# Retention in three parts: queries and keys, values, and the recurrence, with block products through DRAM

## The chip, the cores and the metric

The kernel runs on one core of a Trainium2 chip. The metric is the time on the device in microseconds (us) of one execution. TensorE (PE in the profile) multiplies, VectorE (DVE) and ScalarE (ACT) do elementwise work, GpSimd (POOL) does small things and issues DMAs of its own, SyncE (SP) issues the other DMAs.

## The reference, cut to what matters

One layer of a decoder trunk: 1024 positions, width 1024, all in float32. Both branches of the mixing sub-layer read `u`; the change is in the retention branch (4 heads, queries and keys of 256, values of 512).

```python
hq, hf, hi, hg, rq, rk, rv, rg, ga, gb = jnp.split(u @ w_in[l], split_at, axis=-1)
ya = _hgrn2(hq, hf, hi, hg, lower_bounds[l]) @ w_pa[l]
yb = _retention(rq, rk, rv, rg, positions) @ w_pb[l]
y = (jax.nn.sigmoid(ga) * ya + jax.nn.sigmoid(gb) * yb) @ w_o[l]
x = _layer_norm(DEEPNORM_ALPHA * x + (1.0 + gate1) * y, ln1_g[l], ln1_b[l])
u = x * (1.0 + scale2) + shift2
h = jnp.square(jax.nn.relu(u @ w_up[l] + b_up[l]))
x = _layer_norm(DEEPNORM_ALPHA * x + (1.0 + gate2) * (h @ w_down[l] + b_down[l]), ln2_g[l], ln2_b[l])

def _retention(q, k, v, g, positions):          # q, k rotated by position; per chunk of 128 positions:
    scores = jnp.einsum('bhid,bhjd->bhij', qc, kc) * decay_mask
    o = einsum('bhij,bhje->bhie', scores, vc) + einsum('bhid,bhde->bhie', qc * q_decay, state)
    state = chunk_decay * state + jnp.einsum('bhjd,bhje->bhde', kc * k_decay, vc)
    # then each head's output is centered, normalized and gated by silu(g)
```

## The kernel before

Every large product is float32 made of three: each operand is split by `split` into a part that TensorE reads as fp32r (ACT writes it, tile names ending in h) and a rest (DVE writes it, names ending in l), and `mm3` multiplies h by h, h by l and l by h into one PSUM tile. `u`, transposed, lies split in `uh`, `ul`, as four blocks `ub[j, hf]` (j: half of the width, hf: half of the positions).

The stages follow one another in `build`: `start` (modulation, `u`); the HGRN2 branch, whose dense products `h_dense(p)` are woven with the recurrence `h_pair_rec` of the heads before (`weave` emits steps of two generators in turn), with `gate_proj` of `ga` beside the last; the retention, head by head (`r_head`); `gates` (`gb`, `rg`); `merge`; `out_proj`; `ffn_up`; `ffn_down`.

Each `r_head` projects queries and keys (`dense_T`, 8 times 3 matmuls of 512 columns for one tile), rotates them on DVE, takes the scores of 128 by 128 positions, and then, for each half b of the value width, goes through 8 chunks of 128 positions: `r_v` projects the values of the next chunk (24 matmuls of 256 columns), the state in PSUM (`G`, L901) grows by key times value, and the output (L914) is scores times value plus query times the split state. Columns of the adaptive modulation are summed on DVE beside it (`ada_group`, L424 and L426, two 512 KB loads each, 16 groups in all).

`gates`, `merge`, `ffn_up` and `ffn_down` already use the scheme of Strassen and Winograd: a product of 2 by 2 blocks by seven block products q1 to q7, each on sums of blocks. The sums of the weights of `gb`, `rg`, `pa`, `pb`, `dn` are made in DRAM beforehand by accumulating DMAs (`block_sums`, 8 a part, started by POOL through `start_sums`, one after every so many matmul columns); those of `u` are made by `t_sums` on DVE. `product` and `products` run the block products, `group_out` adds their results up.

Weights come through one stream (`build_stream`, `W`): SP loads pieces of 512 KB into `raw` (three buffers, `raw_bufs`, L316), ACT and DVE split them into `wh`, `wl` (three buffers), and `W` keeps them ahead of the matmuls. The `ada` loads use the same three buffers. The program's order on each engine is set by a scheduler from this code.

## Time and profile before

| what | number |
|---|---|
| median of 3 runs | 2356.52 us (2353.17 to 2358.53) |
| profiled execution | 2359.06 us, of which span 2357.3 us |
| PE, DVE, ACT, POOL busy | 98%, 65%, 38%, 13% |
| mean granted TensorE clock | 0.995 |
| HGRN2 with `ga` | 45 to about 644 us |
| retention | about 644 to 1177 us |
| `gates`, `merge`, `out_proj` | to 1420, 1625, 1740 us |
| `ffn_up`, `ffn_down` | to 2050, 2357 us |

A matmul's row in the profile tells its whole passage through the array, and successive ones overlap; what one costs in a stream is the distance between two starts. DVE and ACT rows overlap only slightly. Every engine works through its own queue in order. Line numbers are those of the kernel before; in the changed kernel they stand a little off.

### The profile page before, as it was taken

The page shows a single profiled execution, that of the slowest core. Times are in us where ns is not written, and L with a number is a line of the kernel's source. Part 1 is how long each engine was busy: PE and PEld are TensorE (multiplying, and loading weights), DVE is VectorE, ACT ScalarE, POOL GpSimd, SP SyncE. Part 2 cuts the span into 40 slices and gives each one's busy share as a digit, 9 for nine tenths or more (in the row PEclk, how much of TensorE's full clock was granted, in tenths as well). Part 3 has the DMA queues.
Part 4 walks back from the last instruction along what each step waited for, and adds up shares of the span by engine and source line. Part 5 has one row for each costly group of instructions (what it writes and reads, how often), then busy time and mean ns, then how long its engine had stood idle before and what let it go on. Part 6 is the DMA issues. An engine that isn't in the chain of part 4 may idle for free.

```text
span 2357.3 us, 31812 instructions
## 1 busy us (share of the span) xinstructions
PE 2299.5 (98%) x12146; PEld 1968.0 (83%) x12146; DVE 1526.5 (65%) x2764; ACT 907.4 (38%) x1447; POOL 313.1 (13%) x479
## 2 busy tenths in 40 slices
PE   7999999999999999999989999999999999999998
PEld 5898888888789898999978878888887888888887
DVE  8356778777274756566576676657787565544678
ACT  4412223232223242424444444442455555544332
POOL 0111122212211121111231111000000000000000
PEclk9999999999999999999999999999999999999999
DMA  9555555545663655546476778776237475865674
GB/s 269 152 137 143 125 141 141 138 120 143 165 188 81 174 139 158 156 123 179 108 251 234 249 259 272 261 262 205 90 116 254 164 251 174 316 206 189 211 237 158
DMA packets 251304, 432.62 MB, mean 184 GB/s; under 512 B 14624, under 2 KB 154128, under 8 KB 245520
## 3 DMA queue, kind: packets, MB, share of 16 engines
q1 hardware_dynamic: 199568, 250.28, 32.9%
q0 software_dynamic: 51264, 179.86, 27.7%
q8 instruction: 95, 1.56, 0.3%
q14 instruction: 57, 0.47, 0.1%
q10 hardware_dynamic: 320, 0.45, 0.1%
HBM read 351.89 MB, written 162.54 MB: 218 GB/s over the span
## 4 chain that ended last, share of the span: by engine, by line
PE 86%; DVE 7%; DMA 4%; ACT 1%; issue 1%; POOL 1%; SPq 0%; DVEq 0%; POOLq 0%; ACTq 0%
PE psd L187 17%; PE psd L189 17%; PE psd L188 17%; PE psc L187 4%; PE psc L188 4%; PE psc L189 4%; PE psa L189 3%; PE psa L188 3%; PE psa L187 3%; PE psa L638 3%; PE psb L914 3%; PE psc L901 2%; PE psb L187 1%; PE psb L188 1%; PE psb L189 1%; DVE wl L183 1%
## 5 line engine op out<-in xcount | busy, mean ns | idle before, releaser
L183 DVE TENSOR_TENSOR wl<-raw,wh 128x1024 fp32r<-128x1024 f32 (+1 forms) x288 | 299.0, 1044 | 236.6 <-ACT wh L182 233.1
L182 ACT ACTIVATE wh<-raw 128x1024 fp32r<-128x1024 f32 (+1 forms) x288 | 262.2, 918 | 417.3 <-PE psd L188 227.5
L187 PE MATMUL psd<-uh,wh 128*128 128x512 f32 x788 | 316.1, 403 | 0.0
L188 PE MATMUL psd<-ul,wh 128*128 128x512 f32 x788 | 312.8, 397 | 0.4 <-DVE ul L183 0.4
L189 PE MATMUL psd<-uh,wl 128*128 128x512 f32 x788 | 313.1, 397 | 0.0
L187 PE MATMUL psd<-wh,uh 128*128 128x256 f32 x768 | 221.2, 288 | 0.0
L189 PE MATMUL psd<-wh,ul 128*128 128x256 f32 x768 | 218.2, 284 | 0.0
L188 PE MATMUL psd<-wl,uh 128*128 128x256 f32 x768 | 218.1, 284 | 0.0
L183 DVE TENSOR_TENSOR hl<-hr,hh 128x1024 fp32r<-128x1024 f32 x96 | 117.3, 1223 | 136.6 <-ACT hh L182 136.6
L188 PEld LDWEIGHTS psd<-ul,wh 128*128 128x128 f32 x788 | 149.0, 189 | 29.0 <-DVE ul L183 1.4
L189 PEld LDWEIGHTS psd<-uh,wl 128*128 128x128 f32 x788 | 148.8, 189 | 28.8
L187 PEld LDWEIGHTS psd<-uh,wh 128*128 128x128 f32 x788 | 148.8, 189 | 28.2 <-ACT uh L182 0.7
L182 ACT ACTIVATE hh<-hr 128x1024 fp32r<-128x1024 f32 x96 | 101.3, 1055 | 182.4 <-PE psb L188 68.0
L187 PEld LDWEIGHTS psd<-wh,uh 128*128 128x128 f32 x768 | 147.0, 191 | 3.0 <-issue 2.6
L188 PEld LDWEIGHTS psd<-wl,uh 128*128 128x128 f32 x768 | 147.0, 191 | 0.3
L189 PEld LDWEIGHTS psd<-wh,ul 128*128 128x128 f32 x768 | 147.0, 191 | 0.0
L645 DVE COPY_PREDICATED hS<-mask,psa 128x128 f32<-128x128 uint8 x288 | 75.8, 314 | 16.7 <-PE psa L638 14.5
L638 PE MATMUL psa<-qp,k 128*128 128x192 f32 x384 | 74.6, 334 | 8.4 <-DVE k L614 8.0
L871 DVE SCALAR_TENSOR_TENSOR vl<-psd,cst,vh 128x256 fp32r<-128x256 f32 x64 | 30.9, 483 | 78.1 <-ACT vh L870 78.1
L638 PEld LDWEIGHTS psa<-qp,k 128*128 128x128 f32 x384 | 63.3, 192 | 17.8 <-issue 14.6
L870 ACT ACTIVATE vh<-psd,cst 128x256 fp32r<-128x256 f32 x64 | 30.3, 473 | 117.5 <-PE psd L189 110.3
L187 PE MATMUL psd<-wh,hh 128*128 128x512 f32 x168 | 65.5, 390 | 0.9 <-ACT o L1405 0.9
(506 smaller groups left out, 5678.5 us busy)
## 6 DMA issues: line engine op xcount, KB each, us to landing
raw<-in_w_in SPq DMA_DIRECT2D x90, 512.0 KB, 4.9
raw<-in_w_up SPq DMA_DIRECT2D x66, 512.0 KB, 5.4
hr<-hv_d SPq DMA_DIRECT2D x56, 512.0 KB, 3.6
dn_s<-in_w_down POOLq DMA_DIRECT2D x48, 512.0 KB, 4.5
hv_d<-hv POOLq DMA_DIRECT2D x16, 1280.0 KB, 5.5
raw<-in_w_ada SPq DMA_DIRECT2D x32, 512.0 KB, 4.8
raw<-dn_s SPq DMA_DIRECT2D x32, 512.0 KB, 4.4
hr<-pv_d SPq DMA_DIRECT2D x28, 512.0 KB, 4.6
```

The source lines that it names most:

```text
L182: self.nc.scalar.activation(hi, src, AF.Copy)
L183: self.nc.vector.tensor_tensor(lo, src, hi.bitcast(F32), op=ALU.subtract)
L187: r = mm(out, wh, uh, start=start, stop=False, skip_group_check=more)
L188: mm(out, wh, ul, start=False, stop=False, skip_group_check=more)
L189: l = mm(out, wl, uh, start=False, stop=stop, skip_group_check=more)
L638: nc.tensor.matmul(pa[:, c * 192:(c + 1) * 192].rearrange("p (b w r) -> p b w r", w=2, r=3 * sz), k[:, n * P:(n + 1) * P], mv, start=True, ...
L645: V.copy_predicated(dst, self.mask8[:, o:o + 128].rearrange("p (b two s) -> p b two s", two=2, s=sz), src)
L870: nc.scalar.activation(hi, pd, AF.Copy, scale=sc)
L871: nc.vector.scalar_tensor_tensor(lo, pd, sc, hi.bitcast(F32), op0=ALU.mult, op1=ALU.subtract)
L901: mm(G[e], l[:, n % 2, es], r, start=n == 0 and i == 0, stop=i == 2, skip_group_check=n > 0)
L914: mm(po, l, r, start=i == 0, stop=i == len(pairs) - 1)
```

## The change

Queries and keys of all four heads are now one block product (`r_qk`: names `rq`, `rk`, 28 steps of 24 matmuls of 512 columns), rotated in `qk_block` (six DVE operations of 512 columns for each pair of an even and an odd tile) and written to DRAM (`qk_d`). Then the values of all heads follow (`r_values`: `rv0`, `rv1`, again 28 steps of 24), scaled and written to DRAM (`v_d`), with the 16 `ada_group`s beside them. Then `r_rec` runs the recurrence from these arrays by 256 positions: `r_prep(i)` loads, splits, transposes and scores one half of a head's positions while `r_main` does the half before. The weight sums of the four new products are 64 more DMAs in `block_sums`: 160 are started from the HGRN2 stage on (before: 96) and 64 later. The sums of `u` are made twice, by `u_sums` in `r_qk` and in `gates`, the second time with one block (`u12`) read back from DRAM. The rotation's angles (`rotary`) move from the second and third pair of HGRN2 heads to the first dense products.

```diff
+ADA_STEPS = (0, 1, 3, 5)
+QK_STEPS = group_steps([(n, p) for n in ("rq", "rk") for p in range(2)])
...
-    def r_qk(self, h):
-    def r_scores(self, h, hf):
-    def r_v(self, h, t, w):
-    def r_head(self, h):
-    def r_norm(self, h, n, of):
...
+    def qk_block(self, s, name, j, n, k, src, sign):
+        nc, V = self.nc, self.nc.vector
+        p, g = divmod(j, 2)
+        if src is s["X"]:
+            r = self.o_tile()
+            nc.scalar.activation(r, src, AF.Copy, scale=sign)
+            src, sign = r, 1.0
...
+        d = self.qk_d[name, 2 * n + p, k]
+        nc.gpsimd.dma_start(d[0], te)
+        nc.gpsimd.dma_start(d[1], to)
+    def r_qk(self, close_u12):
         nc = self.nc
+        self.grp, self.act = {}, {"q1": self.ub[0, 0], "q2": self.ub[1, 0], "q3": self.ub[1, 1]}
+        self.even = {}
+        fo, pl, rot = ExitStack(), ExitStack(), ExitStack()
+        self.fo, self.o_bufs = self.pool("fq", "right", fo), 9
+        plp = self.pool("pl", "right", pl)
+        ra, rb = (plp.tile([P, 8, 512], F32, name="ru" + c) for c in "ab")
+        def get_b12(d):
+            self.whole(d, *self.ub[0, 1])
+            nc.gpsimd.dma_start(self.u12_d.rearrange("k p t -> p k t"), d)
+            close_u12()
+        var = self.u_sums(ra, rb, get_b12)
+        for n, (q, name, p) in enumerate(QK_STEPS):
+            for s, j, pd in self.product(q, name, p):
+                self.group_out(q, s, name, j, pd, self.qk_block, defer=name == "rq")
+            if n < 6:
+                next(var, None)
+            if n == 5:
+                drain(var)
+                pl.close()
...
+                nc.gpsimd.dma_start(self.cos, self.cos_d)
+                nc.gpsimd.dma_start(self.sin, self.sin_d)
+                self.tp = rotp
+        rot.close()
+        fo.close()
+    def r_values(self):
         nc, V = self.nc, self.nc.vector
+        self.ada_acc = []
+        with ExitStack() as s:
+            vp = self.pool("v", "right", s)
+            z3 = [vp.tile([P, 4, 512], F32, name=f"vz{j}") for j in range(3)]
+            z = lambda n, k, i: z3[n + k][:, i]
+            banks = self.bank_sets()
+            step = [0]
+            for a in (0, 1):
+                def done(n, k, i, src, sign, a=a):
+                    h, t = 2 * a + n, 4 * k + i
+                    sc = self.cst[:, K_VSC + h * 8 + t:K_VSC + h * 8 + t + 1]
+                    if sign > 0:
+                        nc.scalar.activation(src, src, AF.Copy, scale=sc)
+                    else:
+                        r = vp.tile([P, 512], F32, tag="vt", bufs=2, name=self.uid("vt"))
+                        V.tensor_scalar(r, src, sc, -1.0, op0=ALU.mult, op1=ALU.mult)
+                        src = r
+                    nc.gpsimd.dma_start(self.v_d[h, t // 2][t % 2 * P:t % 2 * P + P, :], src)
+                def each():
+                    if step[0] % 7 in ADA_STEPS:
+                        self.ada_group(*ADA_ORDER[len(self.ada_acc)])
+                    step[0] += 1
+                self.products(f"rv{a}", 2, MERGE_ORDER, (banks[1], banks[0]), z, done, True, each=each, stop=a == 1, acts=True)
     def ada_group(self, sec, g):
-        raws = self.W(("ada", sec, g))
-        acc = self.rp.tile([P, 256], F32, tag="adacc", bufs=4, name=self.uid("acc"))
+        raws = self.W(("ada", sec, g), ahead=0)
+        acc = self.ac.tile([P, 256], F32, name=self.uid("adacc"))
...
+    def r_load(self, i):
+        if i < 2 * RH:
+            for what in ("rk", "rq"):
+                t = self.rt(what, (P, 2, 512), 2)
+                self.nc.sync.dma_start(t, self.qk_d[what, i // 2, i % 2].rearrange("e p t -> p e t"))
+                self.r_raw[what, i] = t
+    def v_load(self, m):
+        if m < 4 * RH:
+            t = self.wp.tile([P, 2, 512], F32, tag="raw", bufs=self.raw_bufs, name=self.uid("vr"))
+            self.nc.sync.dma_start(t, self.v_d[m // 4, m % 4].rearrange("(t p) c -> p t c", p=P))
+            self.r_raw["v", m] = t
+    def v_split(self, m):
+        if m < 4 * RH:
+            hi, lo = (self.wp.tile([P, 2, 512], F32R, tag="w" + c, bufs=3, name=self.uid("v" + c)) for c in "hl")
+            self.split(hi, lo, self.r_raw.pop(("v", m)))
+            self.v_parts[m] = (hi, lo)
+    def r_prep(self, i):
+        if i >= 2 * RH:
+            return
+        nc, V = self.nc, self.nc.vector
+        self.r_load(i + 1)
+        kf, qf = self.r_raw.pop(("rk", i)), self.r_raw.pop(("rq", i))
+        k = [self.rt("k" + c, (P, 2, 512), 1, F32R) for c in "hl"]
+        q = [self.rt("q" + c, (P, 2, 512), 2, F32R) for c in "hl"]
+        kn, sc = [], []
+        self.r_half[i] = (q, kn, sc)
+        def turn(m):
+            if (i % 2, m) == (1, 1):
+                return None
...
+        def keep(pb):
+            if pb is not None:
...
+        pb = turn(0)
+        self.split(*k, kf)
+        yield
+        keep(pb)
+        pb = turn(1)
+        self.split(*q, qf)
+        yield
+        keep(pb)
+        yield
+        pa = scores(0)
+        yield
+        masked(pa)
+        pa = scores(1)
+        yield
+        masked(pa)
+        yield
+    def r_main(self, i):
+        nc, mm = self.nc, self.nc.tensor.matmul
+        h, hf = divmod(i, 2)
+        q, kn, sc = self.r_half.pop(i)
+        for pr in (0, 1):
+            m = 2 * hf + pr
+            self.v_load(4 * h + m + 2)
+            self.v_split(4 * h + m + 1)
+            if 4 * h + m >= 4 * RH - 2:
+                self._split_to(self.w_next + 4 * h + m + 3 - 4 * RH)
+            vh, vl = self.v_parts.pop(4 * h + m)
+            ns = []
+            if m == 0:
+                self.G = [self.ps("c"), self.ps("c")]
+            if m < 3:
+                kh, kl = kn[pr]
+                for e in (0, 1):
+                    es = slice(e * P, (e + 1) * P)
+                    for c in (0, 1):
+                        for j, (l, r) in enumerate(((kh, vh), (kl, vh), (kh, vl))):
...
+                    t = [self.rt(f"g{c}{e}", (P, 512), 2, F32R) for c in "hl"]
+                    self.split(*t, self.G[e])
+                    ns.append(t)
+                yield
+            sh, sl = sc[pr]
+            for c in (0, 1):
+                po = self.ps("d")
+                pairs = []
+                for b, o in ((0, 128 * c), (1, 256))[:c + 1]:
+                    os = slice(o, o + P)
+                    pairs += [(sh[:, os], vh[:, b]), (sl[:, os], vh[:, b]), (sh[:, os], vl[:, b])]
+                cs = slice((2 * pr + c) * P, (2 * pr + c + 1) * P)
+                if m > 0:
+                    for e in (0, 1):
+                        gh, gl = self.gs[e]
+                        pairs += [(q[0][:, e, cs], gh), (q[1][:, e, cs], gh), (q[0][:, e, cs], gl)]
+                for j, (l, r) in enumerate(pairs):
+                    mm(po, l, r, start=j == 0, stop=j == len(pairs) - 1)
+                self.r_norm(h, 2 * m + c, po)
+                self.ada_end()
+                self.tick()
+                yield
+            self.gs = ns
+    def r_norm(self, h, n, po):
+        nc, V = self.nc, self.nc.vector
+        small = self.rt("small", (P, 16), 4)
+        b6, mv, rs, nb = small[:, 0:6], small[:, 6:8], small[:, 8:9], small[:, 9:10]
+        V.bn_stats(b6, po)
+        V.bn_aggr(mv, b6)
+        V.tensor_tensor(rs, mv[:, 1:2], self.epso[:, h * 8 + n:h * 8 + n + 1], op=ALU.add)
+        nc.gpsimd.tensor_tensor(rs, rs, self.mhalf[:, :1], op=ALU.pow)
+        V.scalar_tensor_tensor(nb, mv[:, 0:1], -1.0, rs, op0=ALU.mult, op1=ALU.mult)
+        on = self.rt("on", (P, 512), 4)
+        nc.scalar.activation(on, po, AF.Identity, scale=rs, bias=nb)
+        self.later(3, lambda: self.r_out(h, n, on))
...
-                var = self.t_sums(*(place[b] for b in ("b11", "b12", "b21", "b22")), whole)
+                var = self.u_sums(ra, rb, lambda d: nc.gpsimd.dma_start(d, self.u12_d.rearrange("k p t -> p k t")))
...
     k.sums = []
     wv = {}
-    for name, w, cut, n in (("gb", w_in[:, C_GB:C_GB + 1024], 1, 2), ("rg", w_in[:, C_RG:C_RG + 2048], 1, 4),
+    for name, w, cut, n in (("rq", w_in[:, C_RQ:C_RQ + 1024], 1, 2), ("rk", w_in[:, C_RK:C_RK + 1024], 1, 2),
+                            ("rv0", w_in[:, C_RV:C_RV + 1024], 0, 2), ("rv1", w_in[:, C_RV + 1024:C_RV + 2048], 0, 2),
+                            ("gb", w_in[:, C_GB:C_GB + 1024], 1, 2), ("rg", w_in[:, C_RG:C_RG + 2048], 1, 4),
                             ("pa", ins["w_pa"], 0, 2), ("pb", ins["w_pb"], 0, 4), ("dn", ins["w_down"], 0, 8)):
         wv[name] = k.block_sums(name, w, cut, n)
     parts = lambda q, name, p: k.spec_1(wv[name][q][p].rearrange("(k p) c -> p k c", p=P), (q, name, p))
+    for q, name, p in QK_STEPS:
...
+    ada = iter(ADA_ORDER)
+    for n, (a, q, p) in enumerate((a, q, p) for a in (0, 1) for q in MERGE_ORDER for p in (0, 1)):
+        specs.append(parts(q, f"rv{a}", p))
+        if n % 7 in ADA_STEPS:
+            sec, g = next(ada)
+            c0 = sec * D + 256 * g
+            pcs = [ins["w_ada"][512 * i:512 * i + 512, c0:c0 + 256].rearrange("(k p) c -> p k c", p=P) for i in (0, 1)]
+            specs.append((pcs, [(("ada", sec, g), [(None, 0, None), (None, 1, None)])]))
...
-    k.start_sums(96, 16 * 512)
+    k.start_sums(160, 10 * 512)
     k.hst = {}
-    k.rot = k.rotary()
     with ExitStack() as s:
...
-        drain(k.h_dense(0))
+        weave(k.h_dense(0), k.rotary(), 13, 24)
         for p in range(4):
             nxt = k.h_dense(p + 1) if p < 3 else k.gate_proj("ga", k.ga_d)
             weave(nxt, k.h_pair_rec(p), 16, 36 if p < 3 else 80)
-            if p == 2:
-                drain(k.rot)
+    k.start_sums(64, 40 * 512)
+    k.r_qk(u12pool.close)
     rs = ExitStack()
-    rotp = k.pool("rot", "right", rs)
-    k.cos = rotp.tile([P, T], F32, name="cos")
-    k.sin = rotp.tile([P, T], F32, name="sin")
-    tc.nc.sync.dma_start(k.cos, k.cos_d)
-    tc.nc.sync.dma_start(k.sin, k.sin_d)
-    assert not k.prep
-    k.start_sums(64, 24 * 512)
-    k.rst = {}
+    k.ac = k.pool("ac", "right", rs)
+    k.r_values()
+    k.close_ta()
+    k.tv.close()
     k.rp = k.pool("r", "right", rs)
-    for h in range(RH):
-        drain(k.r_head(h))
-    late, fo = k.gates(rs.close, u12pool.close)
+    k.r_rec()
+    late, fo = k.gates(rs.close)
...
```

Three places in the programs' order. On PE, before, the value product of one chunk (`psd`) runs into the state (L901, `psc`) and the output (L914, `psb`) of that chunk, and into the next chunk's product:

```order
L188 MATMUL psd_6251<-wl_6208,uh_222 128x256
L189 MATMUL psd_6251<-wh_6207,ul_223 128x256
L901 MATMUL psc_6219<-vh_6247,knh_6042 128x256
L901 MATMUL psc_6219<-vh_6247,knl_6043 128x256
L901 MATMUL psc_6219<-vl_6248,knh_6042 128x256
L901 MATMUL psc_6220<-vh_6247,knh_6042 128x256
```

On PE in the changed kernel the last value product (into `psb_7123`) is followed by transposes of keys (`rk`) that were loaded from DRAM, and these by the state (L1043) and scores (`psa_8358`):

```order
L191 MATMUL psb_7123<-wh_8261,ul_290 128x512
L976 MATMUL psa_8336<-cst,rk_8308 128x128 x4
L976 MATMUL psa_8347<-cst,rk_8308 128x128 x4
L1043 MATMUL psc_8402<-vh_8324,knh_8343 128x512
L1043 MATMUL psc_8403<-vh_8324,knh_8343 128x512
L189 MATMUL psa_8358<-qh_8334,kh_8332 128x256
```

Nothing of the values stands between recurrence rows any more: one seam joins the two parts. On SP, before, four `ada` loads stand among the four of the next half's value weights:

```order
L316 DMA raw_6385<-in_w_ada 128x4x256
L316 DMA raw_6511<-in_w_ada 128x4x256
L316 DMA raw_6685<-in_w_ada 128x4x256
L316 DMA raw_6687<-in_w_ada 128x4x256
L316 DMA raw_6689<-in_w_in 128x4x256
L316 DMA raw_6691<-in_w_in 128x4x256
L316 DMA raw_6869<-in_w_in 128x4x256
L316 DMA raw_6871<-in_w_in 128x4x256
```

On SP in the changed kernel, at the end of the value part (`rv_s`, `in_w_in`: weights and sums for the values), with the first loads of the recurrence (`vr`: values, `rk`, `rq`: keys and queries) behind:

```order
L317 DMA raw_8099<-in_w_in 128x2x512
L317 DMA raw_8101<-rv_s_0_194 128x2x512
L317 DMA raw_8137<-in_w_ada 128x4x256
L317 DMA raw_8179<-in_w_ada 128x4x256
L317 DMA raw_8185<-rv_s_1_195 128x2x512
L317 DMA raw_8187<-in_w_in 128x4x256
L317 DMA raw_8259<-in_w_in 128x4x256
L949 DMA vr_8312<-v_d_143 128x2x512
L949 DMA vr_8314<-v_d_144 128x2x512
L949 DMA vr_8396<-v_d_145 128x2x512
L949 DMA vr_8482<-v_d_146 128x2x512
L943 DMA rk_8308<-rk_d_135 128x2x512
```

All `ada` loads of the layer now pass through this one part, and the first keys (`rk_8308`) are loaded into memory that the value part's results (`vz`) held.

On DVE, before, the sums of `u` (L1123, into `ru`) stand once, behind the last outputs of the retention (`of`), at the start of `gates`:

```order
L932 TENSOR_SCALAR of_11065<-of_11065,small_11563 128x512
L434 SCALAR_TENSOR_TENSOR mod<-psa_11604,cols 128x2
L434 SCALAR_TENSOR_TENSOR mod<-psa_11624,cols 128x2
L183 TENSOR_TENSOR wl_11712<-raw_11386,wh_11711 128x1024
L1123 TENSOR_TENSOR ru_11679<-uh_226,ul_227 128x1024 x2
L1123 TENSOR_TENSOR ru_11678<-uh_220,ul_221 128x1024 x2
```

On DVE in the changed kernel a first set of them (L821, into `rua`, `rub`) stand right behind the last output of the HGRN2 recurrence (L700), while PE still has dense products of `ga` to do; the rows around them split weights (L185):

```order
L700 TENSOR_TENSOR ot_5687<-psb_5682,g_3926 128x512
L185 TENSOR_TENSOR wl_5721<-raw_5264,wh_5720 128x512
L185 TENSOR_TENSOR wl_5721<-raw_5266,wh_5720 128x512
L821 TENSOR_TENSOR rub<-uh_291,ul_292 128x1024 x2
L821 TENSOR_TENSOR rua<-uh_285,ul_286 128x1024 x2
L1129 TENSOR_TENSOR rua<-rua,rub 128x1024 x2
L821 TENSOR_TENSOR rua<-uh_289,ul_290 128x1024
L185 TENSOR_TENSOR q5l_5978<-rua,q5h_5977 128x1024 x2
```

DVE's work on the sums of `u` thus begins beside `ga`; it is there a second time at the start of `gates`.

More of the change, by code (lines that the diff above doesn't have):

```diff
@@ L1081, in take, with gates @@
         return h
[L1083 to L1086 removed]
+    def gates(self, close_r):
+        nc = self.nc
         self.grp, self.act = {}, {"q1": self.ub[0, 0], "q2": self.ub[1, 0], "q3": self.ub[1, 1]}
@@ L1172, in bank_sets, with products @@
                 [self.ps("a"), self.ps("a"), self.ps("c"), self.ps("c")])
-    def products(self, name, parts, order, banks, z, done, w_moves, hold=0, each=None, stop=False):
+    def products(self, name, parts, order, banks, z, done, w_moves, hold=0, each=None, stop=False, acts=False):
         V, A = self.nc.vector, self.nc.scalar
@@ L1215, in products @@
                 w = self.W((q, name, p), k=2, ahead=ahead)
-                self.h_split(self.h_base + parts * n + p + (ahead if tail else 2))
-                h = self.h_parts.pop(0)
+                if acts:
+                    h = [x[:, 2 * p:2 * p + 2] for x in self.act[q]]
+                else:
+                    self.h_split(self.h_base + parts * n + p + (ahead if tail else 2))
+                    h = self.h_parts.pop(0)
                 if each:
@@ L1239, in products @@
             todo.pop(0)()
-        self.h_base += parts * 7
+        if not acts:
+            self.h_base += parts * 7
     def merge(self):
```

287 lines of the change are left out of this document (116 added, 171 removed).

## The prediction

> **What bounds the kernel now.** First the page, then the retention by stretches (the first 33 us of the first one are still `ga`), then single matmuls in the timeline, then the groups of that stage.
>
> ```profile
> PE 2299.5 (98%) x12146; PEld 1968.0 (83%) x12146; DVE 1526.5 (65%) x2764; ACT 907.4 (38%) x1447; POOL 313.1 (13%) x479
> PE 86%; DVE 7%; DMA 4%; ACT 1%; issue 1%; POOL 1%; SPq 0%; DVEq 0%; POOLq 0%; ACTq 0%
> ...
> 611.00:770.00 159.00, 158.22 (x1011) 142.80 (x1010) 80.97 (x164) 46.78 (x98) 24.20 (x38) 1.00 0.54 151
> 770.00:905.00 135.00, 133.76 (x916) 122.30 (x915) 80.23 (x167) 45.81 (x96) 25.41 (x38) 1.00 0.56 149
> 905.00:1041.00 136.00, 136.00 (x934) 125.53 (x933) 82.53 (x174) 44.80 (x94) 25.57 (x37) 1.00 0.56 147
> 1041.00:1177.00 136.00, 134.52 (x948) 124.83 (x947) 82.59 (x167) 51.23 (x103) 25.41 (x36) 1.00 0.57 149
> ```
>
> The columns of the stretches are length, then busy PE, weight loads, DVE, ACT, POOL, the granted clock, the DMA share, GB/s. PE is busy 562.5 of the 566 us, and the chain lies on PE for 86%. So the retention costs what its matmuls cost, and they are priced by the distance of starts:
>
> ```profile
> 640.14 0.39 PE L187 MATMUL psd<-uh,wh 128*128 128x512 f32 x1
> 649.66 0.39 PE L187 MATMUL psd<-uh,wh 128*128 128x512 f32 x1
> ...
> 721.77 0.28 PE L188 MATMUL psd<-wl,uh 128*128 128x256 f32 x1
> 723.93 0.28 PE L188 MATMUL psd<-wl,uh 128*128 128x256 f32 x1
> ...
> 696.33 0.27 PE L189 MATMUL psa<-rqh,rkl 128*128 128x128 f32 x1
> 698.67 0.27 PE L189 MATMUL psa<-rqh,rkl 128*128 128x128 f32 x1
> ...
> L187 PE MATMUL psd<-wh,uh 128*128 128x256 f32 x512 | 147.2, 288 | 0.0
> L901 PE MATMUL psc<-vh,knl 128*128 128x256 f32 x112 | 31.7, 283 | 0.0
> L914 PE MATMUL psb<-gl,rqh 128*128 128x256 f32 x112 | 31.8, 284 | 0.0
> L914 PE MATMUL psb<-vh,sl 128*128 128x256 f32 x64 | 18.1, 283 | 0.0
> ```
>
> The first pair encloses 42 steps: 0.2267 us for 512 columns. The second encloses 18: 0.120 for 256, more than half. The third encloses 21: 0.111 for 128 columns, hardly less than for 256. The groups give the numbers: the value product is three groups like the first (512 each, 1536), the state three like the second (336), the output three like the third and three like the fourth (528).
>
> **The change: matmuls.** Values: 1536 x 0.120 = 184.3 us go, 28 steps x 24 x 0.2267 = 152.3 come: -32.0. Queries and keys: by the code 32 tiles of 24, 768 x 0.2267 = 174.1, become 152.3: -21.8. State and output: 864 x 0.120 = 103.7 become 144 + 288 matmuls of 512, 97.9: -5.8. Scores: 192 x 0.111 = 21.3 become 96 of 256 and 96 of 128, 22.2: +0.9. Sixteen fewer transposes at about 0.1: -1.5. Sum on PE: -60.2. The 3.5 us that PE was idle in the four stretches belonged to waits that go with the old code: -3.5.
>
> **Rotation.** Its 60 us of small DVE operations leave the HGRN2 heads, where PE waited for DVE:
>
> ```profile
> PE psa L638 <- DVE k L614: 8.0, 4, 3.3
> 45.00:175.00 130.00, 129.38 (x762) 113.87 (x762) 69.29 (x171) 40.84 (x73) 20.45 (x28) 1.00 0.61 154
> ```
>
> Half of the 8.0 I take as gained (bounds 0 and -8): -4. Where they go, DVE is idle half the time, so they cost nothing; without that cover they would be late for the first heads. The sums started there rise from 96 to 160, beside weight loads that have two tiles (22 us) of lead: 0 to +5, I take +1 below.
>
> **Queries and keys.** DVE gets 28 weight splits, 24 sums of `u`, 24 additions and 96 operations of the rotation:
>
> ```profile
> L183 DVE TENSOR_TENSOR wl<-raw,wh 128x1024 fp32r<-128x1024 f32 x20 | 24.4, 1221 | 15.4 <-ACT wh L182 15.3
> L806 DVE TENSOR_TENSOR t<-psd,cos 128x512 f32<-128x512 f32 x16 | 11.0, 688 | 10.5 <-PE psd L189 10.5
> L426 DVE SCALAR_TENSOR_TENSOR acc<-raw,cond,acc 128x256 f32<-128x256 f32 x112 | 54.2, 484 | 8.0 <-DMA raw<-in_w_ada 4.7
> ```
>
> 52 x 1.22 + 120 x 0.69 = 146 us for 152 us of PE, but the order puts the sums of `u` under the last `ga` products (33 us). So PE stays ahead: 0 to +8, I take +2.
>
> **Values: the loads.** 28 weight and 32 `ada` loads now pass three buffers in 152 us, one per 2.54 us, so a buffer must turn in 7.6 us. What a turn holds:
>
> ```profile
> raw<-in_w_ada SPq DMA_DIRECT2D x32, 512.0 KB, 4.8
> raw<-pb_s SPq DMA_DIRECT2D x16, 512.0 KB, 5.0
> adw<-in_w_ada SPq DMA_DIRECT2D x16, 512.0 KB, 6.5
> q0 software_dynamic: 12416, 39.86, 34.1%
> q1 hardware_dynamic: 33264, 33.03, 20.9%
> SPq L316 <- DVE acc L426: 120.2, 32, 9.6
> L182 ACT ACTIVATE wh<-raw 128x1024 fp32r<-128x1024 f32 x21 | 22.2, 1057 | 36.4 <-issue 17.0 <-PE psd L188 15.1 <-PE psd L189 4.3
> ```
>
> Landing 4.8, issue 0.4, use 2 (four operations of 0.48 for `ada`, 1.06 and 1.22 for a weight), waiting behind other DVE work some 0.8: 8.0 us, so 60 x 8.0 / 3 = 160 us. SP waited for this very release before (the 120 us row), at a quarter of the rate. The two queue rows are of 500 us (650 to 1150): a load takes all 16 engines 20.9% x 500 / 63 = 1.66 us, a sum at most 34.1% x 500 / 63 = 2.7. Here 60 loads, about 16 sums (one per 42 matmuls) and 8 MB of stores (32 of 256 KB at some 0.8) make 100 + 40 + 25 = 165 us: the DMA engines are full, where landing rose to 6.5 (the row of the start, `adw`). Bounds: 0 (all hidden) and +38 (a turn of 9.5 us: 190 us). I take +14, nearer the low landing, since loads that lag also thin the traffic. The Trainium skill (DMA: Bandwidth & Descriptors, Specifications) gives a core about 358 GB/s from HBM; estimated by that page, some 61 MB read and written here take 170 us, +18, of the same kind as my term.
>
> **The seam.** After the last value matmul nothing is left for PE: result added (DVE 0.7), scaled (ACT 0.6), stored, and only then are keys loaded over the same memory.
>
> ```profile
> or_d<-ot POOLq DMA_DIRECT2D x32, 256.0 KB, 3.6
> hr<-pv_d SPq DMA_DIRECT2D x28, 512.0 KB, 4.6
> 1187.18 0.73 PE L188 MATMUL psd<-q6l,wh 128*128 128x512 f32 x2 [1.50 <-DVE q6l L183]
> 1192.91 0.79 PE L189 MATMUL psd<-q6h,wl 128*128 128x512 f32 x1 [5.00 <-DVE wl L183]
> 1193.50 0.63 PE L187 MATMUL psd<-q6h,wh 128*128 128x512 f32 x1
> 1197.66 0.61 PE L188 MATMUL psc<-q5l,wh 128*128 128x512 f32 x1
> 1198.58 0.39 PE L188 MATMUL psc<-q5l,wh 128*128 128x512 f32 x1
> 1193.00:1195.00 2.00, 2.00 (x5) 1.61 (x6) 2.00 (x2) 0.00 (x0) 0.00 (x0) 0.50 0.39 109
> ```
>
> 0.7 + 0.6 + 3.6 + 4.6 and some 0.5 of signals are 10 us; then splits of 1 us each before the scores can start, about 2; and the clock: before, a wait of 5 us was followed by 5 us at a clock of 0.50, about 12 matmuls with 0.43 between starts in place of 0.23, a loss of 2.4. Sum +14 (bounds 9, were the stores already down, and 18). The Trainium skill (TensorE: Matmul & The Clock Gate, Part 1) says that PE falls to half clock after an idle window of about 3.4 us; the trace agrees, and by that rule shorter waits, as I expect in the value part, cost only themselves.
>
> **Recurrence.** PE has 98 + 22 + about 18 for 176 transposes, some 142 us with `ada`'s few. DVE: 32 splits of 1024 (39 us), 36 of 512 (25), 32 of 384 columns at about 0.55 (18) and 32 norms:
>
> ```profile
> L928 DVE BATCH_NORM_STATS2 small<-of 128x6 f32<-128x512 f32 x32 | 22.2, 694 | 16.5 <-ACT of L918 16.5
> L941 ACT ACTIVATE ot<-psa 128x512 f32<-128x512 f32 x32 | 19.1, 598 | 8.3 <-DMA or_d<-ot 5.7 <-PE psa L939 2.5
> ```
>
> at 0.7 and three small ones, 37: 119 us, 84%; ACT some 102. Each output holds one of three PSUM tiles through a chain over DVE, POOL, DVE and ACT. That lasts about 4 us where outputs come each 4.4 us. Bounds 0 and +32 (4 us in each of 8 half heads); I take +8.
>
> **`gates` and after.** They start as before, with a block of `u` from DRAM in place of two DVE operations, and get about 38 of the later sums at a DMA share of 0.7 to 0.8 (with the +1 above): 0 to +8, I take +3 in all.
>
> **Sum.** -60.2 - 3.5 - 4 + 2 + 14 + 14 + 8 + 3 = -26.7. The profiled execution took 2359.1 us (its span 2357.3), so 2332; the median of the runs is 2.5 lower, so 2330 us.
>
> **Rivals.** (1) The new waits are mostly hidden: values and recurrence at PE's pace, seam 10 and 5 for all else, 15 in place of 41: 2304. For it speaks that in the profile PE waits almost nowhere; against it the full DMA engines. (2) DVE sets the recurrence's pace, +32 in place of +8: 2354. For it the 84% with a fixed order, against it that 83 of 136 us a head did not delay PE before. (3) Slower: the three buffers set the pace of the values. With the other terms as above the change loses from +41 there, at a turn of 9.7 us, which needs a landing of 6.5; at 10.5 us the part takes 210 us and the kernel 2374. For it the `adw` row, against it 4.8 for the same loads in the stage where they stand now. (4) That the products are not as counted: the order shows the counts, so no chance.
>
> **How the numbers follow.** Likeliest, new waits about 41: 0.45. Rival 1: 0.22. Rival 2: 0.13. A value part slower than I take it but short of the turning point, near 2350: 0.10. Rival 3: 0.10. From 2303 to 2360 the first four hold 0.8 and more after their own spread; the likeliest alone spans 2318 to 2343. About 0.2%, 5 us, is what a measurement can tell from no change; same (2352 to 2361) takes parts of rival 2 and of the fourth case: 0.08; slower 0.11; faster 0.81.
>
> **What would show it.** In the changed kernel's profile: starts 0.227 apart in queries, keys and values; the value part 152 us with few waits, or up to 190 with DVE and PE behind DMA of `raw`; one wait of PE of some 10 us before the first transposes (L976), then a clock of 0.5; the recurrence near 150 us. Wrong would make me: `raw` landing above 6 us, waits spread through the recurrence behind DVE, or a delay in HGRN2 from the denser sums.

## The result, and the profile after

The changed kernel takes 2386.66 us (median of 4 runs, 2384.09 to 2391.19) against 2357.53 us before (2353.17 to 2361.44): 1.0126 times as long, 95% interval 1.0101 to 1.0151. The forecast was 2330 us, 27 less than before; it became 29 more. The profiled execution has a span of 2389.4 us, 32.1 more than the one before; it is the slowest of the four, 4.5 us above their median, so the stages below are that much long in all.

First the page of the changed kernel, the engines' busy time:

```profile
PE 2264.0 (95%) x10738; PEld 1877.9 (79%) x10738; DVE 1568.3 (66%) x2715; ACT 934.7 (39%) x1359; POOL 400.4 (17%) x612
```

PE is busy 35.5 us less than before (2299.5), and its share fell from 98 to 95%: the matmuls went, and about 68 us of waiting came. The stretches tell where (length, then busy PE, weight loads, DVE, ACT, POOL, the granted clock, the DMA share, GB/s); first one row of the kernel before, then the changed one's:

```profile
45.00:130.00 85.00, 84.72 (x478) 73.13 (x478) 38.78 (x92) 32.91 (x56) 13.57 (x19) 1.00 0.68 176
```

```profile
45.00:130.00 85.00, 71.29 (x352) 59.22 (x352) 71.89 (x222) 35.53 (x57) 19.30 (x29) 0.89 0.69 181
...
654.00:807.00 153.00, 152.65 (x674) 126.00 (x673) 108.75 (x146) 50.90 (x63) 28.88 (x47) 1.00 0.77 225
...
807.20:996.00 188.80, 164.40 (x674) 131.06 (x672) 109.67 (x189) 52.77 (x72) 27.09 (x45) 0.95 0.80 248
996.00:1021.00 25.00, 0.41 (x3) 0.12 (x2) 8.38 (x14) 5.84 (x8) 4.54 (x9) 0.55 0.65 209
1021.00:1060.00 39.00, 37.85 (x189) 28.06 (x190) 27.74 (x54) 22.69 (x33) 7.91 (x14) 0.94 0.47 157
```

Queries and keys (654 to 807) run as forecast: 153 us, with PE busy for 152.65. The values (807 to 996) take 189 us for 152 us of matmuls. Then comes a hole of 25 us, and behind it a clock below 1. The first products (45 to 130) lost 13 us of busy PE at a clock of 0.89, while DVE's busy time nearly doubled. The last loss is in `gates` and `merge`; two rows of before, then the same two stages of the changed kernel:

```profile
1185.00:1412.00 227.00, 220.49 (x960) 181.31 (x960) 154.61 (x202) 97.39 (x132) 46.51 (x87) 0.98 0.71 251
1412.00:1636.00 224.00, 219.98 (x963) 181.34 (x961) 146.65 (x157) 98.97 (x108) 16.77 (x32) 0.99 0.77 260
```

```profile
1201.00:1434.00 233.00, 223.18 (x958) 182.27 (x959) 151.66 (x199) 96.39 (x132) 61.05 (x108) 0.97 0.89 292
1434.00:1666.00 232.00, 222.63 (x964) 182.42 (x962) 147.56 (x158) 99.37 (x109) 28.28 (x46) 0.99 0.87 284
```

The same work takes 6 and 8 us longer there, with a DMA share 0.10 to 0.18 higher: POOL issues 35 of the 64 sums of `w_down` in these stages; before, all sums were done by then.

**The start.** What PE waited for up to the end of HGRN2 in the changed kernel (total, times, longest), and DVE's timeline around it, the first and the last of the operations on the angles ahead of the late weight:

```profile
PE psd L191 <- DVE wl L185: 10.8, 1, 10.8
...
PE psa L639 <- DVE k L615: 1.3, 3, 0.4
```

```profile
76.73 0.29 DVE L763 CAST rot<-pos 128x256 f32<-128x256 int32 x1 [0.99 <-DMA pos<-in_positions]
...
92.81 0.28 DVE L751 TENSOR_SCALAR rot<-rot 128x256 f32<-128x256 f32 x1
93.02 0.68 DVE L185 TENSOR_TENSOR wl<-raw,wh 128x512 fp32r<-128x512 f32 x1
```

DVE works on the angles without a gap from 76.7 to 93.0, and the low part of a weight that PE needed at 82.6 stands behind them in its queue. In the heads the wait for `k`, 8.0 us before, is down to 1.3: the forecast gain came, 6.7 us, and the price stood elsewhere.

**The hole before the recurrence**, in the changed kernel's timeline, by engine: SP's loads, ACT, POOL's stores, PE.

```profile
985.30 1.80 SPq L317 DMA_DIRECT2D raw<-in_w_in  x2
989.73 9.38 SPq L949 DMA_DIRECT2D vr<-v_d  x2
1006.96 6.56 SPq L949 DMA_DIRECT2D vr<-v_d  x2
1016.64 0.36 SPq L943 DMA_DIRECT2D rk<-rk_d  x1
...
995.99 1.06 ACT L184 ACTIVATE vh<-vr 128x1024 fp32r<-128x1024 f32 x1 [7.55 <-DMA vr<-v_d]
1004.62 1.06 ACT L184 ACTIVATE vh<-vr 128x1024 fp32r<-128x1024 f32 x1 [7.57 <-DMA vr<-v_d]
1005.58 0.70 ACT L901 ACTIVATE vz<-vz,cst 128x512 f32<-128x512 f32 x1
...
1009.67 1.07 POOL L906 DMA_DIRECT2D v_d<-vz  x2
...
1020.91 1.94 PE L976 MATMUL psa<-cst,rk 128*128 128x128 f32 x8 [24.59 <-DMA rk<-rk_d]
```

At 985 SP loads the first two weights of `gates`, which are wanted 190 us later, into two of the three raw buffers. Through the one that is left the value blocks of the recurrence pass singly: the second is issued at 998.7, when the first is split. ACT's queue has the splits of both ahead of the last scalings (L901), so ACT stands until 1004.6, the last stores are issued at 1010, and the key load, which stands in SP's queue behind four value loads and lies over the value results, starts at 1016.6.

### The profile page after: what moved, and what is told of

It is laid out like the page before. It is cut to its first block, busy times and chain, and to the rows that moved or that the text cites. A ratio compares the mean times of both kernels' runs of the same rounds, so it can differ in the third digit from the quotient of the medians.

```text
span 2389.4 us, 29315 instructions
## 1 busy us (share of the span) xinstructions
PE 2264.0 (95%) x10738; PEld 1877.9 (79%) x10738; DVE 1568.3 (66%) x2715; ACT 934.7 (39%) x1359; POOL 400.4 (17%) x612
## 4 chain that ended last, share of the span: by engine, by line
PE 38%; DMA 6%; DVE 5%; issue 2%; ACT 1%; POOL 1%; SPq 0%; DVEq 0%; POOLq 0%; ACTq 0%
PE psd L191 6%; PE psd L189 6%; PE psd L190 6%; PE psc L189 3%; PE psc L191 3%; PE psc L190 3%; PE psa L190 2%; PE psa L191 2%; PE psa L189 2%; DMA raw<-rg_s 1%; PE psb L189 1%; PE psb L191 1%; PE psb L190 1%; DVE wl L185 1%; DMA hr<-pv_d 1%
## 5 line engine op out<-in xcount | busy, mean ns | idle before, releaser
L185 DVE TENSOR_TENSOR wl<-raw,wh 128x1024 fp32r<-128x1024 f32 (+1 forms) x296 | 326.8, 1106 | 242.7 <-ACT wh L184 237.6
L191 PE MATMUL psd<-uh,wl 128*128 128x512 f32 x560 | 225.1, 403 | 10.8 <-DVE wl L185 10.8
L189 PE MATMUL psd<-uh,wh 128*128 128x512 f32 x560 | 226.5, 407 | 3.4 <-DVE o L1214 2.1
L190 PE MATMUL psd<-ul,wh 128*128 128x512 f32 x560 | 226.0, 404 | 0.4 <-DVE ul L185 0.4
L185 DVE TENSOR_TENSOR hl<-hr,hh 128x1024 fp32r<-128x1024 f32 x96 | 117.2, 1222 | 145.9 <-ACT hh L184 145.7
L189 PE MATMUL psd<-wh,uh 128*128 128x256 f32 (+1 forms) x304 | 94.3, 311 | 4.6 <-ACT wh L184 2.9
L190 PE MATMUL psd<-wl,uh 128*128 128x256 f32 (+1 forms) x304 | 93.8, 309 | 3.4 <-DVE wl L185 3.4
L191 PE MATMUL psd<-wh,ul 128*128 128x256 f32 (+1 forms) x304 | 93.6, 308 | 0.0
L1437 POOL TENSOR_TENSOR rs<-rs,mhalf 128x1 f32<-128x1 f32 x16 | 11.9, 747 | 371.8 <-DVE rs L1436 342.6
L427 DVE SCALAR_TENSOR_TENSOR adacc<-raw,cond,adacc 128x256 f32<-128x256 f32 x112 | 53.7, 484 | 20.3 <-DMA raw<-in_w_ada 17.5
L191 PE MATMUL psd<-wh,hl 128*128 128x512 f32 x168 | 65.4, 389 | 0.0
L189 PEld LDWEIGHTS psd<-wh,uh 128*128 128x128 f32 x304 | 59.5, 196 | 7.5 <-ACT wh L184 3.3
L190 PE MATMUL psd<-wl,hh 128*128 128x512 f32 x168 | 65.4, 389 | 0.0
```

Source lines behind the costliest of these rows:

```text
L185: self.nc.vector.tensor_tensor(lo, src, hi.bitcast(F32), op=ALU.subtract)
L189: r = mm(out, wh, uh, start=start, stop=False, skip_group_check=more)
L190: mm(out, wh, ul, start=False, stop=False, skip_group_check=more)
L191: l = mm(out, wl, uh, start=False, stop=stop, skip_group_check=more)
L427: self.nc.vector.scalar_tensor_tensor(acc, w, sc, acc, op0=ALU.mult, op1=ALU.add)
L1437: nc.gpsimd.tensor_tensor(rs, rs, self.mhalf[:, :1], op=ALU.pow)
```

## The experiments

Stages in us, from the starts of PE's rows: the end of the last HGRN2 transposes; the value part; the wait before the first key transposes; from there to the first `q6` product of `gates`; `gates` and `merge`; output projection and up product. (Before: 609.5, then 575.5 to the first `q6` product, 451.3, 406.4.)

| kernel | HGRN2 end | values | wait | to `q6` | gates+merge | out+up | time |
|---|---|---|---|---|---|---|---|
| changed | 621.0 | 188.6 | 25.0 | 180.0 | 466.0 | 408.4 | 2386.7 |
| a1_rot: angles back | 614.4 | 188.4 | 24.5 | 179.7 | 462.2 | 404.8 | 2381.4 |
| a2_cap: no gate weights ahead | 622.6 | 190.3 | 20.3 | 179.3 | 460.7 | 407.5 | 2382.2 |
| a4_sums: down sums moved | 620.2 | 165.6 | 20.6 | 183.9 | 449.6 | 410.7 | 2355.6 |
| b1_adaop: `ada` operations cut | 619.1 | 190.8 | 25.7 | 179.3 | 462.4 | 407.9 | 2388.6 |
| d4_dense: down sums twice as dense | 625.6 | 212.5 | 26.4 | 179.7 | 455.0 | 407.0 | 2406.0 |
| d2_two: a2 + keys not over the values | 623.5 | 189.6 | 2.6 | 191.0 | 458.7 | 408.0 | 2374.8 |
| e2_bufonly: a2 + two `ada` buffers | 622.7 | 180.9 | 11.9 | 179.4 | 463.7 | 407.7 | 2365.7 |
| d3_adabuf: e2 + a4 | 620.6 | 166.6 | 10.0 | 180.3 | 447.6 | 409.5 | 2339.4 |
| d1_all: a1 + a4 + d2 | 609.6 | 165.2 | 1.4 | 190.4 | 448.1 | 411.1 | 2336.9 |
| e1_best: d1 + two `ada` buffers | 612.6 | 168.3 | 0.2 | 184.6 | 448.9 | 409.6 | 2329.4 |

Each row is one profile, and a stage that two runs share does not take the same time in both: the end of HGRN2 lies between 619.1 and 625.6 in the eight with the changed kernel's code for it, the values take 188.4 to 190.8 in the five with its loads and sums, `gates` and `merge` 458.7 to 466.0 in the six with 35 sums there.

**Angles back (a1_rot).**

```diff
-        weave(k.h_dense(0), k.rotary(), 13, 24)
+        k.rot = k.rotary()
+        drain(k.h_dense(0))
 # in h_pair_rec:
+                if p in (1, 2) and n % 3 == 1:
+                    next(self.rot, None)
```

> The rotation's angles are made in the second and third pair of HGRN2 heads again, as before the change; all else as changed. Theory A: made beside the first dense products they put two sines into ACT's queue ahead of the weight splits, and PE waits for a weight's low part (10.8 us at 82.6, 13.5 us of waiting more in the first 130 us than before, with the clock about 17), of which some 6 come back as shorter waits in the heads: 2376 us (-11), the start's wait gone, the heads' waits back to 12. Rival: the first weights are late because the denser weight sums (one per 12 matmuls) take the DMA engines there: the wait stays, 2387 us.

2381.38 us, ratio to before 1.009 (1.0071 to 1.0109). The start's wait is gone, and PE's wait for `k` is back:

```profile
45.00:130.00 85.00, 84.31 (x476) 72.59 (x475) 39.07 (x96) 33.68 (x57) 19.81 (x27) 1.00 0.85 208
```

```profile
PE psa L640 <- DVE k L616: 7.9, 3, 6.2
```

Theory A holds as to the place: with sums just as dense (DMA share 0.85 against 0.68 before) PE is busy 84.3 of 85 us again, so the rival falls. In the queue it named the rows differ: it was DVE's, as shown above, not ACT's. The gain up to the end of HGRN2 is 6.6 us between these two profiles, not 11; over all profiles, the eight with the early angles end HGRN2 at 621.9 on the mean and the three with late ones (a1_rot, d1_all, e1_best) at 612.2, so some 10 us. What these three lose against before (4.9, 0.1 and 3.1 us) is within what the runs scatter, so the price of the denser sums in HGRN2 stays open.

**No gate weights ahead (a2_cap).**

```diff
-        while self.w_load < min(n, len(self.w_pcs)):
+        while self.w_load < min(n, len(self.w_pcs), self.load_cap):   # up to the last value weight in r_values
```

> Weight loads stop at the last value weight until the recurrence begins: the first two weights of the gates no longer lie in two of the three raw buffers from 985 us on. Theory B: with one buffer left, the second load of values waits for the split of the first, ACT's queue holds that split ahead of the last four scalings, and SP's queue holds two more such loads ahead of the first keys; so PE's wait of 24.6 us falls to about 14: 2376 us. Rival: the wait is the recurrence's pool lying over the value results, whose last stores land as late as before: 24 us remain, 2387 us.

2382.20 us, ratio 1.0093 (1.0074 to 1.0112). The wait fell from 25.0 to 20.3 us, not to 14: three raw buffers bring the value blocks 7 us earlier (the second split at 997.6 in place of 1004.6), but the last scalings then wait for DVE until 1003.9 and the key load for the stores until 1015.0. DVE was late because it, too, stood, for the store of a result in one of the two `vt` buffers:

```profile
999.60 0.75 DVE L904 TENSOR_SCALAR vt<-psc,cst 128x512 f32<-128x512 f32 x1 [5.52 <-DMA v_d<-vt]
```

So both theories held a part, and a third cause stood beside them; no run gives `vt` more buffers.

**Down sums moved (a4_sums).** No sums in values, `gates` and `merge`.

```diff
+    k.pace, k.rec_sums = 1 << 30, 24      # ahead of r_values
+    k.pace, k.cols_done = 44 * 512, 0     # ahead of out_proj
 # in r_main, behind each output's last matmul:
+                if self.rec_sums:
+                    self.rec_sums -= 1
+                    self.after(self.prep.pop(0)(), last)
```

> The sums of down weights pause during values, gates and merge; 24 are issued in the recurrence (one behind each output), the rest (31) in the output projection and the up product. Theory C: the sums take DMA time from the loads: the 16 us lost between the start of gates and the end of the output projection go, and the values fall from 189 to 165 us: 2348 us. Rival D: the values are paced by the turn of the three raw buffers (DVE's four operations on each ada piece and its queue), not by the traffic: only the 16 us go, 2371 us. Either way the up product, now with 31 sums, may lose 0 to 10 us, and the recurrence 0 to 8.

2355.59 us, ratio 0.9987 (0.9976 to 0.9997): 31 us less than the changed kernel. 23.0 us are in the values, 16.4 in `gates` and `merge`, 4.4 in the wait; recurrence and the stages after `merge` pay 6 (the two profiled executions lie 37 us apart, a little more than the medians). The DMA issues of the value part (KB each, median us to landing) in the changed kernel; then this run's stretch and its issues:

```profile
raw<-in_w_ada SPq DMA_DIRECT2D x29, 512.0 KB, 5.5
raw<-rv_s SPq DMA_DIRECT2D x16, 512.0 KB, 5.0
dn_s<-in_w_down POOLq DMA_DIRECT2D x12, 512.0 KB, 6.8
raw<-in_w_in SPq DMA_DIRECT2D x12, 512.0 KB, 6.6
dn_s<-dn_s POOLq DMA_DIRECT2D x3, 512.0 KB, 7.5
```

```profile
807.00:972.50 165.50, 156.96 (x672) 125.83 (x670) 110.11 (x190) 53.88 (x72) 16.58 (x31) 0.99 0.73 238
```

```profile
raw<-in_w_ada SPq DMA_DIRECT2D x29, 512.0 KB, 4.8
raw<-rv_s SPq DMA_DIRECT2D x16, 512.0 KB, 4.3
raw<-in_w_in SPq DMA_DIRECT2D x12, 512.0 KB, 4.6
```

One sum is left in the values here. Without the other 14 each load lands 0.7 to 2.0 us earlier. Theory C holds, rival D falls.

**`ada` operations cut (b1_adaop).**

```diff
-        for k in range(KT):
+        for k in (0, 4):
             self.ada_step(acc, raws[k // 4][:, k % 4, :], k, k == 0)
```

> All 32 ada loads are made, but of the four operations on each piece only the first is done (the modulation is incomplete). Rival D (DVE and the holding time of the buffers pace the values): DVE has 43 us less in the value part, a piece is held 1.5 us instead of 2 to 4, and the part falls from 189 to about 165 us: 2363 us. Theory C (landing times and traffic pace them): still 180 us or more, 2378 to 2386 us.

2388.64 us, ratio 1.0116 (1.0096 to 1.0136), the values 190.8 us. DVE's work fell from 109.7 to 65.3 us there and the part got no shorter. SP's waits in the value part, of the changed kernel and of this one:

```profile
SPq L317 <- DVE adacc L427: 96.4, 40, 8.8
SPq L317 <- DMA raw<-rv_s: 17.2, 6, 7.5
SPq L317 <- DMA raw<-in_w_ada: 14.1, 8, 4.0
```

```profile
SPq L317 <- DMA raw<-in_w_ada: 90.0, 23, 8.0
```

Much the same time is put down to DVE first and, without DVE's work, to the landing of the load: the releaser named was not the cause. The prediction had read the same row of the kernel before (120.2 us) as this very wait.

**Down sums twice as dense in the values (d4_dense).**

```diff
+    k.pace = 20 * 512
     k.r_values()
+    k.pace = 40 * 512
```

> As changed, but the down sums run twice as densely in the value part (one per 21 matmuls, some 28 there in place of 14) and so 14 fewer later. Theory C: a sum costs the values 1.7 us each (23 us for 14 taken away), so the values take 212 us, and what comes after loses 6 less: 2404 us. Rival: the loss in the values is there once the loads have any company, and 14 more change little: 2380 to 2390 us.

2405.97 us, ratio 1.0198 (1.0181 to 1.0215). The values took 212.5 us, with 30 sums in place of 15:

```profile
raw<-in_w_ada SPq DMA_DIRECT2D x29, 512.0 KB, 6.8
dn_s<-in_w_down POOLq DMA_DIRECT2D x23, 512.0 KB, 7.7
...
dn_s<-dn_s POOLq DMA_DIRECT2D x7, 512.0 KB, 8.1
```

1 sum, 165.6; 15 sums, 188.6; 30 sums, 212.5 us: 1.6 us a sum on both legs. Theory C again. `gates` and `merge`, with 19 sums left in place of 35, took 455.0 us: 11 less than in the changed kernel's profile, but 7 less than the mean of the six profiles with 35 (462.3), where 6 were forecast. In the four with none they took 447.6 to 449.6 (mean 448.6): some 0.4 us a sum in these stages.

**Keys and queries not over the value results (d2_two).**

```diff
-        return self.rp.tile(list(shape), dt, tag="r_" + tag, ...)
+        pool = self.rl if tag in ("rk", "rq", "kh", "kl", "qh", "ql", "knh", "knl", "mask3", "epso") else self.rp
+        return pool.tile(list(shape), dt, tag="r_" + tag, ...)
...
+    k.rl = k.pool("rl", "left", rs)
     k.rp = k.pool("r", "right", rs)      # the rest, over the value results
```

> As the run without gate weights ahead (2382 us, wait before the recurrence 20 us), and the keys, queries and their splits lie over the sums of u instead of the value results. Theory B2: of those 20 us all but the split and clock is the key load's wait for the last value stores, which lie under its tiles: PE has transposes and scores to do while they land, the wait falls to 4 to 8 us: 2370 us. Rival: PE then stops a few matmuls later, at the first masked scores and split states, whose tiles still lie over the value results, for nearly the same end: 2378 to 2382 us.

2374.82 us, ratio 1.0067 (1.0052 to 1.0082): 7 less than a2_cap. PE starts almost at once and stops again:

```profile
1002.41 1.06 PE L977 MATMUL psa<-cst,rk 128*128 128x128 f32 x8 [2.18 <-DMA rk<-rk_d]
1011.76 1.22 PE L1044 MATMUL psc<-vh,knh 128*128 128x512 f32 x2 [8.29 <-ACT knh L184]
```

Of the 17.7 us taken from the wait, 11.7 come back behind it (8.3 of them this one, where ACT has splits of values, keys and queries and the last scalings ahead of the transposed keys). So the overlay was a cause, and with it gone the order of ACT's queue is next.

**Two buffers of their own for the `ada` pieces**, beside the sums (e2_bufonly) and without them (d3_adabuf):

```diff
-        t = self.wp.tile([P, 1024], F32, tag="raw", bufs=self.raw_bufs, ...)
+        pool, tag, bufs = (self.vp, "adr", 2) if i in self.ada_pcs and self.vp else (self.wp, "raw", self.raw_bufs)
+        t = pool.tile([P, 1024], F32, tag=tag, bufs=bufs, ...)
...
-                self._load_to(max(i for _, i, _ in ops) + 3)
+                self._load_to(max(i for _, i, _ in ops) + (5 if self.first_v <= self.w_split < self.first_g else 3))
```

> As the run with the down sums moved (2355.6 us; values 166 us where PE's work is 152), without gate weights ahead, and the ada pieces have two buffers of their own beside the three, with loads five pieces ahead. Theory E (the three shared buffers cost what is left of the values' loss): values 155 us, 2340 us (11 less there, 5 less before the recurrence). Rival (the rest is landing time and order, not the number of buffers): values 164 to 168 us, 2351 us.

> As the run without gate weights ahead (2382 us), down sums as changed, and two buffers of their own for the ada pieces. Theory C alone (the sums take the engines' time, the number of buffers is of no account): the values stay at 186 to 190 us, 2372 to 2382 us, the lower end by the shorter wait before the recurrence. Theory E2 (slow landings cost only because the three buffers allow no lead): with five buffers the values fall below 175 us even beside the sums, 2362 us.

d3_adabuf: 2339.43 us, ratio 0.9918 (0.9903 to 0.9932). The time is that of theory E, but not for its reason: the values stay at 166.6 us, as the rival said, and it is the wait that fell, from 20.6 in a4_sums to 10.0 us. Part of that belongs to the gate weights, which are held back here as well (4.7 us in a2_cap); from a2_cap to e2_bufonly, where only the buffers and the lead differ, the wait falls by 8.4. e2_bufonly: 2365.67 us (7 runs, 2360.13 to 2374.33), ratio 1.0035 (1.0019 to 1.0052), the values 180.9 us, between the two theories: beside the sums the longer lead takes back 9 of the 23 us; without the sums it has nothing to take. With landings of 4.3 to 4.8 us (a4_sums) more buffers brought the values nothing, with 5.0 to 6.6 us (changed kernel) they did.

**Four and five edits together (d1_all, e1_best).**

> Four edits together: angles in the heads as before, no gate weights loaded ahead of the recurrence, down sums paused in values, gates and merge, and the recurrence's keys, queries and their splits in a pool of their own over the sums of u (not over the value results). If the parts add up: 2387 - 6 (angles) - 5 (gate weights) - 31 (sums) - 11 (keys no longer behind the last value stores) = 2334 us, faster than before by 1%. Rival: the gains overlap, since all of them shorten the same waits for DMA: 2345 to 2352 us.

> The four edits together (2337 us) and two buffers of their own for the ada pieces. In the run with these buffers the values took 166 us as without, but the wait before the recurrence was 10 us shorter. If that came from value loads and splits that stand earlier, much of it is already had by the pool that no longer waits for the stores: 2330 to 2336 us. If it adds up whole: 2327 us. Rival: the two act on the same wait, 2337 us.

d1_all: 2336.94 us, ratio 0.9902 (0.9887 to 0.9917): the parts add up to within 3 us. e1_best: 2329.44 us, ratio 0.9883 (0.9865 to 0.9901), a version faster than both kernels, by 28 and 57 us. The rival (2337 us) falls; the time lies between the two other cases, next to that in which much of the gain is had already. Its value part, and what is left of the wait at the seam:

```profile
799.50:967.70 168.20, 157.77 (x672) 127.36 (x671) 116.53 (x202) 58.36 (x76) 18.12 (x35) 0.98 0.76 253
```

```profile
972.45 0.80 PE L1047 MATMUL psc<-vh,knh 128*128 128x512 f32 x1 [3.48 <-ACT knh L184]
```

## Why the prediction was wrong

By its own steps, forecast first, then the profile:

- **Matmuls, -60.2 and -3.5: right, and small.** From the end of HGRN2 to the first `q6` product it is 575.5 us before and 579.9 after. New in it are 36.3 us in the values (188.6 for 152.3), 25.0 of the wait, 16.2 in the recurrence (180.0 less 21.8 for the 96 matmuls of `gates` ahead of `q6`, forecast 142) and 0.7 in queries and keys, 78 in all; so 74 us went, 10 more than counted. By the starts in the trace before, the old groups were some 7 us dearer than one pair of each had said: the 1536 value matmuls took 187 us for 184, state and output 105 for 104, and matmuls of 512 columns stood 0.230 apart for 0.2267. The other 3 are no gain: the matmuls of `ada` in the 142 were taken at 4 us and took 7.
- **Rotation, -4: wrong.** The gain was there (8.0 to 1.3 us) and the step priced it; "where they go, DVE is idle half the time, so they cost nothing" failed. An engine idle on the mean can still have 16 us of work in one piece ahead of the one operation that PE waits for. Up to the end of HGRN2 the change cost 11.5 us.
- **Queries and keys, +2: right**, +0.7.
- **Values, +14 with bounds 0 and 38: the choice within the bounds failed**, +36.3. The buffer turned in 188.6 x 3 / 60 = 9.4 us, as the upper bound had it. The step took the low end "since loads that lag also thin the traffic"; but the number of sums goes by the count of matmuls, 15 in the part however long it lasts, and 14 of them at 1.6 us are 23 of the 36 us (a4_sums, d4_dense). The other 13 us stay with one sum and three or five buffers (a4_sums, d3_adabuf): in a4_sums 8.5 of them are waits of PE and the rest slow starts behind these. So +14 is about what the loads cost without the sums, though it was worked out with them: that the size fits is luck. The use by DVE, which the turn also held, was of no account (b1_adaop). The step's own second sum was a little low as well: 16 sums at 2.7 are 43 us, not 40. The estimate by the Trainium skill (DMA: Bandwidth & Descriptors, Specifications), 170 us, was of the same kind and as low: its 61 MB in 188.6 us are 323 GB/s, so the page's 358 was not reached (the profile, which counts a transfer's bytes once, reads 46.8 MB and 248 GB/s at a DMA share of 0.80).
- **Seam, +14 with bounds 9 and 18: outside its bounds**, 25.0, and a clock of 0.94 in the 39 us behind. The chain of result, store and load was added up with every step starting at once. Two queues were left out: SP's, where value loads through one free buffer stood ahead of the keys, and ACT's, where their splits stood ahead of the last scalings. The listing of SP's order ahead of the prediction shows four `vr` loads ahead of `rk`; it was read for what waits on the stores, not for what stands in front. The gate weights in the raw buffers were 4.7 us of the wait (a2_cap), DVE's own stand for the `vt` stores was left out too, and with the keys off the value results another 17.7 went, of which 11.7 came back behind (d2_two).
- **Recurrence, +8: low**, 16, but not by rival 2: PE waited 4.1 us in it. The rest is the clock behind the seam and starts more than the counted distance apart (state and output take 105 us for 98, `ada`'s matmuls 7 for 4).
- **`gates` and after, +3: wrong**, `gates` and `merge` +14.7 (+11.0 by the mean of the six profiles), output projection and up product +2.0. Some 38 sums, 35 by the trace, in stages at a DMA share of 0.71 and 0.77 were taken to fit in the rest; a4_sums took 16.4 us back by moving 31 of them into stages at 0.32 and 0.64, where they cost 2.3 us, and the other 4 into the recurrence.

Added up as the profiles have it, -73.9 + 11.5 + 0.7 + 36.3 + 25.0 + 16.2 + 14.7 + 2.0 make +32.5, against 32.1 us measured. The sum had a wrong sign at the rotation and was too low at four more places: values, seam, recurrence, `gates` and after. Rival 3 had the right sign for a reason of the right kind (landing at 5.0 to 6.6 us), but gave the value part alone the power to turn the result; it turned because the same sums of weights were dear in three stages, and because what stands in front of a step in its queue was left out, on DVE at the start, on SP and ACT at the seam. The range, to 2360, had no room for that: its slower cases move one term at a time and keep the others as forecast.

## What to carry to other kernels

Work that is "in the background" of DMA has a price per piece in each stage where loads run just in time; find it by moving the pieces to a stage with slack (here output projection and up product), and the price is the difference: 1.6 us a sum in the values, some 0.4 in `gates` and `merge`, about 0.1 in output projection and up product. Before a store-and-reload seam is priced, read what stands in front of its steps in each queue, prefetches for later stages above all: they hold the buffers that the seam needs. And the mean load of an engine says nothing of one operation behind a long block on it.

## What the runs showed of the hardware

The loss per sum was the same from 1 to 15 and from 15 to 30 sums (1.64 and 1.59 us), at mean DMA shares of 0.73, 0.80 and 0.86. The mean hides full stretches. Here the value part is cut into 40 slices of 4 to 5 us, each digit a slice's DMA share in tenths (9 is 90% or more), in a4_sums, in the changed kernel and in d4_dense:

```profile
DMA  9686867958777488887898947568947284585895
```

```profile
DMA  8599698978797767799898946966999645948597
```

```profile
DMA  7797799959889994999589979984799939998799
```

With 1, 15 and 30 sums 6, 15 and 23 of the 40 read 9. Share times length gives 121, 151 and 183 us of all 16 engines' time, so a sum took an estimated 2.1 us of it, and 1.6 were paid.

Short waits cost more than themselves. In the value part of the changed kernel one wait of 5.2 us was followed by this:

```profile
959.72 0.80 PE L190 MATMUL psd<-wl,q5h 128*128 128x512 f32 x1 [5.23 <-DVE wl L185]
960.32 0.63 PE L191 MATMUL psd<-wh,q5l 128*128 128x512 f32 x1
960.74 0.63 PE L189 MATMUL psd<-wh,q5h 128*128 128x512 f32 x1
```

```profile
959.60:962.00 2.40, 2.28 (x5) 1.82 (x6) 2.26 (x6) 0.00 (x0) 0.00 (x0) 0.50 0.49 176
```

Starts 0.43 apart for 4.8 us, 2.3 us lost. Four waits of 2.9 to 3.5 us there lost 1.5 to 1.7 us each in the same way, those of 0.8 to 2.0 us only 0.1; of the 36 us in the values, 24 are waits and some 12 the slow starts behind them. The length alone does not decide: in b1_adaop waits of 2.20 and 2.30 us lost 1.7 us each, and waits of 2.97 and 3.20 us only 0.1. The forecast had taken waits below 3.4 us as costing only themselves, by the Trainium skill (TensorE: Matmul & The Clock Gate, Part 1). The page also says that the window runs freely, and these waits show that less than its length can be enough.
